# Turning q and k in three units instead of one, with q's second copy made by a transfer inside SBUF

## Chip, cores and metric

The kernel runs on one core of a Trainium2 chip (trn2). The metric is the device time of one execution in microseconds (us); of the kernel before it is the median of three runs.

## What is computed

One residual block over 4096 tokens of width 1024: a norm with a scale and shift from a conditioning vector, one projection into q, k, v, u and z, chunked attention over q, k, v, a trailing pool over u, a gate by silu(z), and an output projection. The change lies in the attention.

```python
h = rms_norm(x, norm_g) * (1 + scale) + shift
q, k, v, u, z = split(h @ w_in)          # q, k, v: 8 heads of 64
q = rms_norm(q, q_norm_g); k = rms_norm(k, k_norm_g)
# a chunk of 64 tokens attends to itself and to 8 chunks left of it
s = einsum('bqhd,bkhd->bhqk', qn, kn) * scale + bias
a_out = einsum('bhqk,bkhd->bqhd', softmax(s), vn)
y = concat([a_out, p_out]) * silu(z)
x = x + gate * (y @ w_out)
```

The inputs are float32. Each matmul operand is kept as a high part and a low part (the rest), both in the format fp32r, and a product is made of three matmuls: high by high, high by low, low by high.

## The kernel before

The program has three parts. From 0 to about 600 us the input is normed and transposed, u, z and the pool are made, and h goes to HBM as `hT_d`. From about 600 to 1730 us the attention runs. What is left of the output projection follows.

**Units.** The attention has two phases of four heads each; a phase has eight groups of 512 tokens. A unit `u` is one head on one group: 64 units, and group g of the 16 (both phases counted through) has the units 4g to 4g+3. The loop over `u` merges three lists of work into one order: the second half of unit u (probabilities transposed on TensorE, L623, cast to a high part on ScalarE, L629, and a low part on VectorE, L630, multiplied with v, L641 and L642), the first half of unit u+1 (scores, L583 and L584, into one PSUM tile `sps` that has no second buffer; bias and minimum on VectorE, L588; exponent on ScalarE, L601), and `work`, mostly one projection block of 128 tokens of a later group (L495 to L497). A projection block loads its h by SP (L105) and splits it (L96 on ScalarE, L97 on POOL); its q and k are normed by POOL and VectorE and stay in `qkr` tiles of the pool `b_qk`. The scheduler of the language then reorders the instructions and gives every engine one fixed order.

**Turns.** The scores need q and k with the 64 head dimensions on the partitions. `tq(which, pair)` does that for a pair of heads and one group, and is called a turn here: four transposes on TensorE (L537) of four `qkr` tiles into one PSUM tile, then for both heads (`s0`, `s1`: the two halves of the partitions)

```python
qs[s0] = copy(ps[s0])                    # L545, ScalarE, for q
qs[s1] = copy(ps[s0])                    # L546, ScalarE, the same values into the other half
ql[s0] = ps[s0] - qs[s0]                 # L548, VectorE, low part
ks[s0] = copy(ps[s0]); ks[s1] = ps[s0] - ks[s0]   # L556 ScalarE, L557 VectorE, for k
```

k's high part stands in one half of the partitions and its low part in the other, so one matmul with `qs` in both halves (L583) adds q-high by k-high and q-high by k-low; L584 with `ql` adds the third product. L583 therefore reads both copies of q. A group has four turns (q and k of two pairs). They stand in unit 4g-2, put into the projection block's items at every fifth place, and are ready for unit 4g, whose scores are made in the merged work of unit 4g-1.

**Buffers.** k lies in a ring of three slots of 512 tokens for each head; `slot` is the group modulo 3. A score tile covers 640 keys: where the group's slot is not the first of the ring, these lie side by side, and it is made of two pieces of 320 columns; where it is the first, of two pieces that together have 640 columns and whose sizes depend on the tile (512 and 128 for the first). `qs` has two buffers, `ql` one (two for the last head).

**Queues.** Every DMA that the program issues in the attention part stands in SP's queue, in order: loads of h (L105), loads of the gate tile z (L649), stores of y (L334), the bias (L461), and at the ends of the two phases the next weights (L125 and L139 for the projection, L408 for the output). An instruction that waits in that queue holds those behind it. A load of h into the staging buffer `bhr` (two buffers) waits until L97 has read the one before.

## Time and profile before

| | |
|---|---|
| median of three runs | 1998.72 us (1996.77 to 2001.21) |
| the profiled execution | 1996.48 us |
| its span, first to last instruction | 1994.6 us |
| mean granted clock of TensorE | 0.998 of full speed (2.4 GHz) |
| busy share of the span: TensorE matmuls | 97% |
| busy share: VectorE / ScalarE / POOL | 57% / 47% / 43% |

PE stands for TensorE's matmuls, PEld for its weight loads, which run beside matmuls; DVE is VectorE, ACT ScalarE, SP the engine that issues the DMAs. Matmuls are pipelined, and a PE row's ends are modelled. A window row gives a stretch of the trace: its bounds and length in us, then for each engine busy us and the number of instructions, the granted clock (1.00 is full speed), and the DMA share.

### The profile page before, as it was taken

How to read it: one execution, taken by the hardware profiler on the slowest of the kernel's cores; microseconds unless marked ns; L12 is line 12 of the kernel's file. 1: busy time of each engine (PE TensorE's matmuls, PEld its weight loads, DVE VectorE, ACT ScalarE, POOL GpSimd, SP SyncE). 2: the span in 40 equal slices, each digit the busy share in tenths (PEclk: the TensorE clock that was granted, in tenths of full speed). 3: DMA queues.
4: the chain of work that ended last, by engine and by line, in shares of the span. 5: the costliest groups of instructions: out<-in, count | busy, mean ns of one | idle time of the engine just before them, and what ended most of it. 6: DMA issues, size and time to landing. Idle time of an engine off the chain costs nothing.

```text
span 1994.6 us, 30020 instructions
## 1 busy us (share of the span) xinstructions
PE 1930.3 (97%) x10544; PEld 1657.0 (83%) x10544; DVE 1143.5 (57%) x2331; ACT 934.8 (47%) x1974; POOL 851.5 (43%) x1424
## 2 busy tenths in 40 slices
PE   6989999999999999999999999999999999999999
PEld 5778888888888888889888888898889788888887
DVE  7655654465635656666677666666666754333323
ACT  4422212221325656665678566756675864310121
POOL 7231332033045644445445656354445554422243
PEclk9999999999999999999999999999999999999999
DMA  9555344444431111111113222111111344544454
GB/s 331 192 174 159 103 135 145 141 123 141 148 101 53 59 58 33 44 54 43 54 52 97 74 60 64 33 59 38 43 54 43 101 142 139 180 136 149 146 181 164
DMA packets 167112, 211.76 MB, mean 106 GB/s; under 512 B 16432, under 2 KB 92720, under 8 KB 166960
## 3 DMA queue, kind: packets, MB, share of 16 engines
q1 hardware_dynamic: 166960, 209.84, 32.7%
q8 instruction: 83, 1.36, 0.3%
q14 instruction: 69, 0.57, 0.1%
HBM read 151.05 MB, written 58.74 MB: 105 GB/s over the span
## 4 chain that ended last, share of the span: by engine, by line
PE 85%; ACT 6%; DMA 3%; DVE 2%; POOL 2%; issue 2%; SPq 0%; ACTq 0%; POOLq 0%; DVEq 0%
PE ps L495 9%; PE ps L496 9%; PE ps L497 8%; PE ps L430 6%; PE ps L428 6%; PE ps L429 6%; PE ptps L623 5%; PE aps L297 4%; PE aps L298 4%; PE aps L296 4%; PE ps L297 4%; PE ps L298 4%; PE ps L296 4%; PE ops L641 3%; PE ops L642 3%; PE sps L583 3%
## 5 line engine op out<-in xcount | busy, mean ns | idle before, releaser
L97 POOL TENSOR_TENSOR bhl<-bhr,bhh 128x512 fp32r<-128x512 f32 x212 | 275.0, 1297 | 321.5 <-ACT bhh L96 313.5
L495 PE MATMUL ps<-w,bhh 128*128 128x512 f32 (+1 forms) x1024 | 353.6, 345 | 4.8 <-ACT qkr L508 4.6
L496 PE MATMUL ps<-w,bhh 128*128 128x512 f32 (+1 forms) x1024 | 352.5, 344 | 0.0
L497 PE MATMUL ps<-w,bhl 128*128 128x512 f32 (+1 forms) x1024 | 352.4, 344 | 0.0
L630 DVE TENSOR_TENSOR ptl<-ptps,pth 128x512 fp32r<-128x512 f32 x480 | 226.3, 486 | 145.6 <-ACT pth L629 142.1
L96 ACT CAST bhh<-bhr 128x512 fp32r<-128x512 f32 x224 | 138.9, 620 | 291.5 <-PE ps L429 184.9
L629 ACT CAST pth<-ptps 128x512 fp32r<-128x512 f32 x480 | 193.1, 425 | 147.2 <-PE ptps L623 132.3
L588 DVE CUSTOM_DVE_ANT_0 p<-sps,nb 128x640 f32<-128x640 f32 (+4 forms) x256 | 199.1, 778 | 86.4 <-PE sps L584 81.0
L601 ACT ACTIVATE p<-p,mx 128x640 f32<-128x640 f32 (+4 forms) x256 | 204.5, 799 | 90.7 <-DVE mx L588 89.6
L495 PEld LDWEIGHTS ps<-w,bhh 128*128 128x128 f32 x1024 | 193.7, 189 | 26.1 <-ACT qkr L508 7.9
L623 PE MATMUL ptps<-ident,p 128*128 128x128 f32 x1200 | 208.0, 274 | 3.5 <-DVE ql L548 2.9
L496 PEld LDWEIGHTS ps<-w,bhh 128*128 128x128 f32 x1024 | 193.7, 189 | 17.8
L497 PEld LDWEIGHTS ps<-w,bhl 128*128 128x128 f32 x1024 | 193.6, 189 | 17.2
L428 PE MATMUL ps<-w,bhh 128*128 128x512 f32 x512 | 200.6, 392 | 1.0 <-ACT bhh L96 1.0
L430 PE MATMUL ps<-w,bhl 128*128 128x512 f32 x512 | 200.3, 392 | 0.6 <-POOL bhl L97 0.6
L429 PE MATMUL ps<-w,bhh 128*128 128x512 f32 x512 | 200.2, 391 | 0.0
L259 POOL TENSOR_TENSOR xt<-xt,rb 128x512 f32<-128x512 f32 x56 | 80.0, 1463 | 234.2 <-DMA rb<-rs_d 234.2
L583 PE MATMUL sps<-kr,qs 128*128 128x320 f32 (+2 forms) x480 | 156.6, 334 | 13.0 <-DVE mx L588 12.3
L623 PEld LDWEIGHTS ptps<-ident,p 128*128 128x128 f32 x1200 | 144.3, 140 | 22.4 <-DVE ql L548 4.2
L641 PE MATMUL ops<-pth,v 128*128 128x512 f32 x480 | 157.7, 329 | 5.0 <-ACT pth L629 4.8
L642 PE MATMUL ops<-ptl,v 128*128 128x512 f32 x480 | 155.6, 334 | 0.1
L297 PE MATMUL aps<-hlo,w 128*128 128x512 f32 x392 | 153.6, 392 | 1.8 <-DVE hlo L97 1.8
(131 smaller groups left out, 3933.1 us busy)
## 6 DMA issues: line engine op xcount, KB each, us to landing
bhr<-hT_d SPq DMA_DIRECT2D x128, 256.0 KB, 2.7
bhr<-yT_d SPq DMA_DIRECT2D x96, 256.0 KB, 2.8
xt<-in_x_dram SPq DMA_DIRECT2D x32, 512.0 KB, 4.9
qkr<-in_x_dram SPq DMA_DIRECT2D x64, 256.0 KB, 3.4
out_dram<-qkr SPq DMA_DIRECT2D x64, 256.0 KB, 2.1
xt<-in_xT_dram SPq DMA_DIRECT2D x28, 512.0 KB, 6.5
hT_d<-xt SPq DMA_DIRECT2D x56, 256.0 KB, 2.3
w_s<-in_w_adaT_dram SPq DMA_DIRECT2D x16, 512.0 KB, 6.7
```

The lines of the kernel that those rows point to most:

```text
L97: eng.tensor_tensor(lo, raw, hi.bitcast(F32), op=ALU.subtract)
L297: nc.tensor.matmul(ps, wh[:, cs], l_, start=False, stop=False)
L428: nc.tensor.matmul(ps, a_, wh, start=k == 0, stop=False)
L429: nc.tensor.matmul(ps, a_, wl, start=False, stop=False)
L430: nc.tensor.matmul(ps, l_, wh, start=False, stop=k == KT - 1)
L495: nc.tensor.matmul(ps, a_, wh, start=k == 0, stop=False)
L496: nc.tensor.matmul(ps, a_, wl, start=False, stop=False)
L497: nc.tensor.matmul(ps, l_, wh, start=False, stop=k == KT - 1)
L583: nc.tensor.matmul(o, QS[ph, sg, h][:, qc], ks[:, k0 : k0 + n], start=True, stop=False)
L623: nc.tensor.transpose(out=ps[:, i * P : (i + 1) * P], in_=Pt[ph, sg, h, i][:, w : w + P], identity=ident)
L630: nc.vector.tensor_tensor(l_[:, r], ps[:, r], a_[:, r].bitcast(F32), op=ALU.subtract)
L641: nc.tensor.matmul(o[:, r], v, a_[:, r], start=n == 0, stop=False, skip_group_check=True)
```

## The change

The turns of a group are taken apart: q and k of pair 0 stay in unit 4g-2, q of pair 1 goes to unit 4g-1, k of pair 1 to unit 4g, by a table `turns`. (Group 0 keeps all four in one block.) q's second copy, ScalarE's L546, becomes a DMA from one half of the SBUF tile to the other, issued by SP: 64 x 512 values of 4 bytes, 128 KB, 64 times. `qs` has one buffer instead of two, the last head's `ql` one instead of two, the ring two slots instead of three; `b_qk` has eight buffers instead of six, since `qkr` tiles live longer. The gate tiles of the output get memory of their own.

```diff
-    op = ctx.enter_context(tc.tile_pool(name="b_qk", bufs=6))
+    op = ctx.enter_context(tc.tile_pool(name="b_qk", bufs=8))
...
-        qp = cb.enter_context(tc.tile_pool(name="b_q", bufs=2))
+        qp = cb.enter_context(tc.tile_pool(name="b_q", bufs=1))
...
-        ring = [kp.tile([P, 3 * SG], F32R, name=f"kr{h}") for h in range(HP)]
-        qlo = [[kp.tile([P, SG], F32R, name=f"ql{h}_{i}") for i in range(2 if h == HP - 1 else 1)] for h in range(HP)]
+        ring = [kp.tile([P, 2 * SG], F32R, name=f"kr{h}") for h in range(HP)]
+        qlo = [kp.tile([P, SG], F32R, name=f"ql{h}") for h in range(HP)]
...
         def slot(ph, sg):
-            return (ph * NSG + sg) % 3
+            return (ph * NSG + sg) % 2
...
                         nc.scalar.activation(qs[s0], ps[s0], AF.Copy, scale=gqn[s0])
-                        nc.scalar.activation(qs[s1], ps[s0], AF.Copy, scale=gqn[s0])
-                        ql = qlo[2 * pair + e][(ph * NSG + sg) % len(qlo[2 * pair + e])]
+                        nc.sync.dma_start(qs[s1].bitcast(F32), qs[s0].bitcast(F32))
+                        ql = qlo[2 * pair + e]
...
-            return [lambda w=w, p=p: tq(w, p) for p in range(2) for w in range(2)]
+            return {(w, p): (lambda w=w, p=p: tq(w, p)) for p in range(2) for w in range(2)}
...
-            if kb[1] >= 4 and kb[1] % 4 == 0:
-                for n, f in enumerate(tq_items(kb[0], kb[1] // 4 - 1)):
-                    it.insert((2 if kb != (0, 4) else 9) + (5 if kb != (0, 4) else 3) * n, f)
+            if kb == (0, 4):
+                t = tq_items(0, 0)
+                for n, wp in enumerate(((0, 0), (1, 0), (0, 1), (1, 1))):
+                    it.insert(9 + 3 * n, t[wp])
             return it
+        turns = {u: [] for u in range(-1, 64)}
+        for g in range(1, 2 * NSG):
+            t = tq_items(g // NSG, g % NSG)
+            turns[4 * g - 2] += [t[0, 0], t[1, 0]]
+            turns[4 * g - 1] += [t[0, 1]]
+            turns[4 * g] += [t[1, 1]]
...
-            if u in (26, 58):
-                work = [none] * 6 + [f for t in tq_items(u // 58, NSG - 1) for f in (t, none, none)] + work
-            if u == 27:
-                work = [none] * 20 + work
+            if u in (26, 27):
+                work = [none] * (16 if u == 26 else 20) + work
+            for n, f in enumerate(turns[u]):
+                work.insert(min(len(work), 3 + 6 * n), f)
...
-                    gate[n] = ring[n][:, SG : 2 * SG].bitcast(F32)
+                    gate[n] = bp.tile([P, 512], F32, name=f"gate{n}")
```

After the change a line behind L471 has the number of the line before less one (the first copy is L544, the transfer L545). Below, the rows that each engine runs in order, of both kernels.

ScalarE (ACT), group 11, from the first copy of q's pair 0 on. `qs00` is q for head 0 of pair 0 and `qs01` for its head 1, `kr0` the ring of head 0, `pth` a high part of probabilities, `p` the exponent, `bhh` the high part of h. Before:

```order
L545 ACTIVATE qs00_14511<-ptps_14506,gqn_4532 64x512
L546 ACTIVATE qs00_14511<-ptps_14506,gqn_4532 64x512
L96 CAST bhh_15320<-bhr_15318 128x512
L629 CAST pth_14529<-ptps_14525 128x384
L601 ACTIVATE p_14556,ls_14504<-p_14556,mx_14557 128x640
L629 CAST pth_14547<-ptps_14544 128x256
L545 ACTIVATE qs01_14515<-ptps_14506,gqn_4532 64x512
L546 ACTIVATE qs01_14515<-ptps_14506,gqn_4532 64x512
L556 ACTIVATE kr0_4534<-ptps_14560,pt_107 64x512
L601 ACTIVATE p_14630,ls_14504<-p_14630,mx_14631 128x640
```

After:

```order
L544 ACTIVATE qs00_14515<-ptps_14510,gqn_4532 64x512
L96 CAST bhh_15318<-bhr_15316 128x512
L544 ACTIVATE qs01_14519<-ptps_14510,gqn_4532 64x512
L628 CAST pth_14478<-ptps_14473 128x512
L628 CAST pth_14490<-ptps_14485 128x512
L600 ACTIVATE p_14499,ls_14502<-p_14499,mx_14500 128x640
L628 CAST pth_14527<-ptps_14523 128x384
L628 CAST pth_14542<-ptps_14539 128x256
L628 CAST pth_14567<-ptps_14563 128x384
L507 COPY qkr_15251<-ps_15168 128x512
L600 ACTIVATE p_14554,ls_14502<-p_14554,mx_14555 128x640
L555 ACTIVATE kr0_4534<-ptps_14599,pt_107 64x512
```

The second copies L546 are gone; casts of probabilities (L628) that stood behind the turn now stand between its copies. The first copy of pair 1 (`qs10_14757`) now stands 26 rows behind that of pair 0, the first copy of k for pair 1 another 18 rows on.

SP's queue at the end of phase 0, where the next phase's weights are loaded (eight loads L125, then four L139). `yT_d` is a store of y, `gzb` a load of the gate tile. Before:

```order
L125 DMA bhr_10949<-in_w_in_dram 128x2x256
L125 DMA bhr_10953<-in_w_in_dram 128x2x256
L125 DMA bhr_10959<-in_w_in_dram 128x2x256
L125 DMA bhr_10963<-in_w_in_dram 128x2x256
L334 DMA yT_d5_90<-osum_10254 128x4x128
L649 DMA gzb_11220<-gz_d6_83 128x512
L139 DMA bhr_10969<-in_w_in_dram 128x2x256
```

After:

```order
L125 DMA bhr_10947<-in_w_in_dram 128x2x256
L125 DMA bhr_10951<-in_w_in_dram 128x2x256
L125 DMA bhr_10957<-in_w_in_dram 128x2x256
L545 DMA qs10_10301<-qs10_10301 64x512
L125 DMA bhr_10961<-in_w_in_dram 128x2x256
L545 DMA qs11_10305<-qs11_10305 64x512
L139 DMA bhr_10967<-in_w_in_dram 128x2x256
```

Between the loads of the weights now stand the two transfers of q's pair 1 of group 6 (`qs10_10301`, `qs11_10305`). At the end of phase 1 the two of group 14 stand in the same way behind ten loads L408.

SP's queue in the turn of group 2, after the change (the `L105` rows before them are loads of h for group 4):

```order
L105 DMA bhr_7455<-hT_d4_73 128x512
L105 DMA bhr_7505<-hT_d4_73 128x512
L545 DMA qs00_6411<-qs00_6411 64x512
L105 DMA bhr_7688<-hT_d4_73 128x512
L334 DMA yT_d1_86<-osum_6126 128x4x128
L545 DMA qs01_6415<-qs01_6415 64x512
L648 DMA gzb_7178<-gz_d2_79 128x512
L545 DMA qs10_6653<-qs10_6653 64x512
L545 DMA qs11_6657<-qs11_6657 64x512
```

Before, the queue has only the rows L105, L334 and L649 here. The transfer `qs00_6411` stands behind two loads L105, each of which waits for a staging buffer. Between the last transpose of this q and the first score matmul that reads it TensorE has 37 instructions in its order; the other groups' counts are 29 (group 0), 43 (group 10) and 73 to 134.

## Rows read from the trace of the kernel before

**Rows 1.** Page, busy time (us), share of the span, instructions, by engine.

```profile
PE 1930.3 (97%) x10544; PEld 1657.0 (83%) x10544; DVE 1143.5 (57%) x2331; ACT 934.8 (47%) x1974; POOL 851.5 (43%) x1424
```

**Rows 2.** Windows: one turn stretch (group 11) and the stretch after it.

```profile
core 0: us, PE busy (x) PEld busy (x) DVE busy (x) ACT busy (x) POOL busy (x), PEclk, DMA share, GB/s
1342.90:1362.10 19.20, 16.70 (x97) 13.41 (x96) 15.84 (x36) 17.59 (x36) 3.79 (x7) 1.00 0.17 50
1362.10:1381.20 19.10, 19.10 (x131) 17.58 (x130) 11.96 (x27) 10.20 (x26) 12.21 (x30) 1.00 0.09 30
```

**Rows 3.** Windows: three of the twelve turn stretches, and the sum of twelve.

```profile
742.70:762.20 19.50, 16.96 (x94) 13.45 (x95) 15.97 (x36) 17.27 (x35) 1.95 (x5) 1.00 0.09 28
...
1210.60:1224.70 14.10, 13.85 (x84) 11.73 (x83) 10.44 (x26) 11.97 (x27) 7.13 (x17) 1.00 0.12 37
...
1548.60:1566.10 17.50, 15.85 (x93) 12.99 (x92) 13.65 (x30) 16.37 (x33) 3.86 (x6) 1.00 0.16 46
sum 221.80, PE 198.93 PEld 162.37 DVE 177.78 ACT 198.61 POOL 51.36; mean PE 16.58 PEld 13.53 DVE 14.82 ACT 16.55 POOL 4.28
```

**Rows 4.** Windows: one of ten stretches between turns, and the sum of ten.

```profile
1362.10:1411.80 49.70, 49.70 (x331) 45.62 (x330) 29.39 (x71) 26.79 (x66) 28.34 (x65) 1.00 0.15 46
...
sum 486.80, PE 485.93 PEld 443.00 DVE 293.22 ACT 272.95 POOL 278.52; mean PE 48.59 PEld 44.30 DVE 29.32 ACT 27.29 POOL 27.85
```

**Rows 5.** Windows: where weights are loaded (two), and between them a turn stretch.

```profile
1036.00:1077.10 41.10, 40.61 (x271) 36.18 (x269) 31.09 (x76) 31.89 (x76) 26.55 (x51) 1.00 0.36 109
1077.10:1099.90 22.80, 22.80 (x144) 20.32 (x142) 16.08 (x31) 18.12 (x34) 13.28 (x25) 1.00 0.22 70
1566.10:1601.70 35.60, 32.69 (x216) 28.61 (x215) 28.00 (x69) 29.57 (x72) 25.03 (x43) 1.00 0.43 133
```

**Rows 6.** Groups by line and shape: the copies and subtractions of the turns.

```profile
L545 ACT ACTIVATE qs<-ptps,gqn 64x512 fp32r<-64x512 f32 x64 | 43.6, 682 | 6.5 <-PE ptps L537 3.6 <-DVE ql L548 1.9
L546 ACT ACTIVATE qs<-ptps,gqn 64x512 fp32r<-64x512 f32 x64 | 43.7, 683 | 0.8
L556 ACT ACTIVATE kr<-ptps,pt 64x512 fp32r<-64x512 f32 x64 | 43.7, 683 | 4.6 <-PE ptps L537 1.9 <-DVE kr L557 1.3
L548 DVE SCALAR_TENSOR_TENSOR ql<-ptps,gqn,qs 64x512 fp32r<-64x512 f32 x64 | 47.9, 749 | 37.5 <-ACT qs L546 37.2
L557 DVE SCALAR_TENSOR_TENSOR kr<-ptps,pt,kr 64x512 fp32r<-64x512 f32 x64 | 48.0, 750 | 11.2 <-ACT kr L556 10.0
```

**Rows 7.** Waits, whole program: engine, line, releaser: us, times, longest.

```profile
DVE ql L548 <- ACT qs L546: 37.2, 41, 2.4
```

**Rows 8.** Groups by line and shape: score matmuls, by columns of a piece.

```profile
L583 PE MATMUL sps<-kr,qs 128*128 128x320 f32 x288 | 93.5, 332 | 8.1 <-DVE mx L588 7.5 <-DVE kr L557 0.3
L584 PE MATMUL sps<-kr,ql 128*128 128x320 f32 x288 | 88.1, 313 | 0.0
L583 PE MATMUL sps<-kr,qs 128*128 128x512 f32 x48 | 21.2, 442 | 1.8 <-DVE mx L588 1.8
L584 PE MATMUL sps<-kr,ql 128*128 128x512 f32 x48 | 18.9, 394 | 0.0
L583 PE MATMUL sps<-kr,qs 128*128 128x128 f32 x48 | 11.9, 248 | 0.0
L584 PE MATMUL sps<-kr,ql 128*128 128x128 f32 x48 | 13.2, 275 | 0.0
```

**Rows 9.** DMA issues: KB each, median us from issue to landing.

```profile
gz_d<-gz SPq DMA_DIRECT2D x32, 256.0 KB, 2.1
gzb<-gz_d SPq DMA_DIRECT2D x32, 256.0 KB, 2.9
```

**Rows 10.** Waits of SP's queue, 600 to 1630 us.

```profile
SPq L105 <- POOL bhl L97: 374.6, 63, 23.0
```

**Rows 11.** Timeline of SP: the end of the first weight loads.

```profile
1019.08 34.36 SPq L125 DMA_DIRECT2D bhr<-in_w_in_dram  x8
```

More of the change, by code (lines that the diff above doesn't have):

```diff
@@ L469, in block_kernel @@
         gk = pt[:, C_GK : C_GK + 1]
-        ring = [kp.tile([P, 3 * SG], F32R, name=f"kr{h}") for h in range(HP)]
-        qlo = [[kp.tile([P, SG], F32R, name=f"ql{h}_{i}") for i in range(2 if h == HP - 1 else 1)] for h in range(HP)]
+        ring = [kp.tile([P, 2 * SG], F32R, name=f"kr{h}") for h in range(HP)]
+        qlo = [kp.tile([P, SG], F32R, name=f"ql{h}") for h in range(HP)]
         for h in range(HP):
             z = slice((1 - h % 2) * HD, (2 - h % 2) * HD)
-            for t_ in qlo[h]:
-                nc.gpsimd.memset(t_[z].bitcast(F32), 0.0)
+            nc.gpsimd.memset(qlo[h][z].bitcast(F32), 0.0)
         def slot(ph, sg):
-            return (ph * NSG + sg) % 3
+            return (ph * NSG + sg) % 2
         Vt, QK, QS, QL = {}, {}, {}, {}
```

## The prediction

> **What bounds the kernel now.** I read the page's busy shares first. TensorE's matmuls fill 97% of the span, and no other engine reaches 60% [rows 1]. By that row at most 3% is left to win, and a reader would stop here. The second view, busy time by stretches, says where this misleads. Two neighbouring stretches of 19 us, cut at the units' borders, both at full clock: in the one without turns TensorE runs 131 matmuls and loads weights for 17.58 us; in the one with group 11's turns, as long, it runs 97 and loads for 13.41 [rows 2]. A weight load's time depends on what is loaded and not on who is late, so its share tells how dense the work is. Over ten stretches between turns it is 443.00/486.80 = 0.910 [rows 4]; there the other engines are at 60% (VectorE), 56% and 57%, and matmuls fill 99.8%. Over twelve turn stretches it is 162.37/221.80 = 0.732 [rows 3]. At the density between turns their work would last 162.37/0.910 = 178.4 us, so the turns cost 221.8 - 178.4 = **43.4 us**, 3.6 each. What holds TensorE there is ScalarE: 17.59 of 19.20 us busy in the example, 198.61 of 221.80 in all (90%), with VectorE next at 80% [rows 2, 3].
>
> By the matmuls' idle time only 221.80 - 198.93 = 22.9 us are lost there [rows 3]. The Trainium skill ("Perfetto Trace Analysis", section "Identifying the Most-Contended Engine") says that matmul busy time is a poor measure of the distance to the limit, since matmuls are pipelined, and that the busy share of weight loads is a better one. This trace agrees: 16.70 against 19.10 us of matmuls, but 97 against 131 of them [rows 2].
>
> **What goes from the turn stretches.** Of a group's turns, ScalarE has 12 copies (4 L545, 4 L546, 4 L556) of 0.683 us, VectorE 8 subtractions of 0.750 us [rows 6]. The four second copies become transfers. Of pair 1, two first copies of q and two copies of k go to the next two units, with four subtractions and eight transposes. So a turn stretch loses 8 x 0.683 = 5.46 us of ScalarE, 4 x 0.750 = 3.0 us of VectorE, and of TensorE 8 x 0.15 = 1.2 us (the pace between turns, 49.70 us for 331 matmuls [rows 4]). Over twelve stretches: ScalarE 198.6 - 65.6 = 133 us, VectorE 177.8 - 36 = 142 us, TensorE 178.4 - 14.4 = 164 us. ScalarE falls to 81% of TensorE's need, VectorE to 86%: TensorE bounds the stretch again, with less slack than elsewhere. The waits of the subtraction for the second copy, 37.2 us in all [rows 7], go too, since in the changed order L547 waits for the first copy alone; they lie inside the 43.4 and are not added.
>
> **What stays lost there.** Nothing before has exactly this load; I bound it by the nearest rows, each with the same 0.910. The turn stretch by the weight loads (ScalarE 79%, VectorE 71%) needs 20.32/0.910 = 22.3 of its 22.8 us, 2% lost; the weights of phase 0 (78% and 76%) 36.18/0.910 = 39.8 of 41.1, 3%; the weights of phase 1 (83%, 79%) 28.61/0.910 = 31.4 of 35.6, 12% [rows 5]; group 8's turn stretch, in which only part of the turns lies (85%, 74%), 11.73/0.910 = 12.9 of 14.1, 9% [rows 3]. I take 9% of 164 = **14.8 us**, since this row is a turn stretch with eight transposes as each will be; ends 3 us (2%) and 20 us (12%). The gain is 43.4 - 14.8 = 28.6 us.
>
> **What the neighbours take.** The two units after the turn get 4 x 0.683 = 2.7 us of ScalarE and 3.0 us of VectorE in each group. Over 49.7 us ScalarE rises from 56% to about 61%, VectorE from 60% to 66%, below every row above that loses time: nothing. TensorE's 1.2 us are moved, not saved. If this cover fails (the scores' single buffer waits for a VectorE that is late), 1% of 487 us is 5 us.
>
> **The ring.** With two slots, 8 groups instead of 9 have their keys side by side (of 14 that have keys to the left; 288 pieces of 320 columns are 9 groups of 16 tiles of 2 pieces [rows 8]). In the other one, 16 tiles take split pieces: 0.442 + 0.394 + 0.248 + 0.275 = 1.36 us for the most uneven against 2 x (0.332 + 0.313) = 1.29. That is at most 16 x 0.07 = 1.1 us; I take 0.6. The buffers that are gone (q, low part, ring slot) hold nobody up in the built order: q of pair 0 is written when heads 0 and 1 of the group before have long been read. The two `qkr` buffers more give room for turns that read later.
>
> **The transfer's latency.** q's first copy used to be followed by the second, 0.68 us; now by a transfer. No row has one inside SBUF; those of 256 KB land 2.1 and 2.9 us after issue [rows 9], and this one is half as large. The first score needs it, and TensorE's 37 instructions between (group 2; 29 and 43 for groups 0 and 10) are 4.4 to 6.5 us of work at 0.15; all other groups have 11 us or more. Copy and landing need 0.7 + 2.9 = 3.6 us, so these three fit if SP issues at once. But the transfer stands behind loads L105, which wait for POOL, 374.6 us in 63 waits: 5.9 us in the mean, 23.0 at most [rows 10]. With a wait of 5.9 us 3.6 + 5.9 = 9.5 us are needed: late by 5.1, 3.9 and 3.0, together 12 us; the others still have room. The loads ahead are freed by TensorE's work 12 to 34 rows before the transposes, so I expect most of the wait to be over: **3 us**, ends 0 and 12.
>
> The Trainium skill ("SBUF — State Buffer", section "Door 1: The DMA port swizzle") has a rule against this part: a transfer of 64 partitions reaches half of the 16 ports. No row shows such a transfer. As an estimate by that page it lasts as long as a full one of twice the size, so one takes the 2.9 us of the 256 KB rather than less, up to 0.8 us more, 2.4 us at the three tight turns.
>
> **The phase ends.** There the transfers of pair 1 stand between weight loads, eight L125 in 34.36 us, 4.3 us for each [rows 11]. q of pair 1 is needed 65 to 113 instructions after its transposes (9.8 to 17 us): two loads ahead are covered, a third is not. I take **3 us** for both ends, ends 0 and 12.
>
> **Sum.** 43.4 - 14.8 - 0.6 - 3 - 3 = 22.0 us off the profiled execution of 1996.48: 1974.5. It stands 2.2 us below the median of the runs, so the forecast for the median is **1976.7 us**. With all low ends it is 1998.7 - 40.4 = 1958; with all high ends 43.4 - 20 - 1.1 - 12 - 12 is a loss of 2, 2000.
>
> **Rivals.**
> - *Nearly all stalls go* (chance 0.09): the turns lose nothing, and the later turn of pair 1 also relieves the weight stretches, which lose 1.3 and 4.2 us now. 43.4 - 1 + 3 = 45: 1953 us. For it: stretches with ScalarE at 79% lose 2% [rows 5].
> - *VectorE takes ScalarE's place* (0.17). It is left with 86% of TensorE's need, 95% in the fuller stretches ((15.84 - 3.0)/(14.7 - 1.2) for group 11 [rows 2]), and the scores wait for it. With 12%, 20 us, left in the turn stretches, 1% in the neighbours (5 us) and 10 us of latency instead of 6: 43.4 - 20 - 5 - 10 - 0.6 = 8 us of gain: 1991.
> - *Matmul idle time is the true measure* (0.06): only 22.9 us could be won, and 22.9 - 14.8 - 6.6 = 1.5: 1997. Against it are the counts of matmuls.
> - *SP's queue decides* (0.10), slower. If the loads ahead wait w at each turn, each transfer is late by 3.6 + w less its room (4.4, 5.6 and 6.5 us for the tight groups, 11 to 20 for the rest). At w = 13 the sum is 62 us over the 16 groups, against 43.4 - 14.8 - 0.6 - 3 = 25 won without it: 37 slower, 2036. It passes no change near w = 9.4, where the lateness is some 26 us. Mean wait 5.9 and longest 23.0 [rows 10] leave this possible; that L105's waits mostly end before the turn's transposes speaks against.
> - That the change does not do what it says is excluded by the built order: 64 transfers in SP's queue, no second copy on ScalarE.
>
> **Numbers.** The forecast's own case has 0.58. Some 0.2% (4 us) is what a measurement of this kernel can tell from no change. Faster by more: forecast, all stalls gone, VectorE, less 0.02 for their upper tails: 0.82. Within 0.2%: the matmul-idle case and those tails, 0.08. Slower: SP's queue, 0.10. The range leaves out the slower rival and half of the fastest, and reaches over the VectorE case to the idle-time case: 1953 to 1998 us.
>
> **What would show it.** Right: in the turn stretches the weight loads' share rises from 0.73 to about 0.83, ScalarE falls from 90% to about 75%; L546's 43.7 us are gone, the wait for the second copy with it; pieces of 320 columns fall from 288 to 256. Wrong: scores waiting for the DMA of `qs` for more than some 6 us in all (SP's queue); scores waiting longer for L588 with VectorE over 90% in the turn units (VectorE); a longer lateness at the two phase ends; or turn stretches as long as before with fewer matmuls.

## The result, and the profile after

The changed kernel takes 1988.79 us (median of 4 runs, 1987.33 to 1990.24) against 1999.53 us of the kernel before beside it (4 runs): a ratio of 0.9948, 95% interval 0.9930 to 0.9965. That is 10.7 us less, where 22 had been forecast: the direction holds and the time lies inside the range, but the gain is half the size. The profiled execution took 1987.33 us, with a span of 1985.0 us, 9.6 less than before.

The page's busy row, which answers to [rows 1]:

```profile
PE 1932.2 (97%) x10544; PEld 1659.5 (84%) x10544; DVE 1139.5 (57%) x2331; ACT 892.0 (45%) x1910; POOL 852.1 (43%) x1423
```

TensorE still stands at 97%. ScalarE has lost 42.8 us, nearly all of the second copies' 43.7, and VectorE 4.0.

Busy time by stretches (the columns as in [rows 2]). First the units 4g-2 of the same twelve groups as in [rows 3], with the example of group 11 and the sum:

```profile
1342.40:1355.00 12.60, 12.06 (x89) 10.91 (x87) 9.73 (x23) 9.20 (x21) 5.91 (x14) 1.00 0.13 42
...
sum 158.80, PE 151.35 PEld 132.32 DVE 124.65 ACT 122.26 POOL 94.02; mean PE 12.61 PEld 11.03 DVE 10.39 ACT 10.19 POOL 7.83
```

At the density of [rows 4] (weight-load time over length) the weight loads need 132.32/0.910 = 145.4 us, so 158.8 - 145.4 = 13.4 us are lost here, where it was 43.4. Now the units 4g-1 behind them, which the prediction had taken for free, after the change: those of groups 6, 8, 11 and 14, then the sum of the twelve.

```profile
1030.20:1048.60 18.40, 16.99 (x99) 14.29 (x99) 13.54 (x32) 15.03 (x36) 6.59 (x6) 1.00 0.40 113
1165.10:1188.30 23.20, 21.57 (x126) 18.45 (x127) 14.87 (x41) 13.84 (x38) 8.19 (x12) 1.00 0.18 50
...
1355.00:1376.60 21.60, 21.32 (x134) 18.76 (x133) 15.93 (x35) 14.73 (x36) 6.64 (x8) 1.00 0.11 29
...
1560.30:1573.00 12.70, 11.19 (x66) 8.72 (x65) 10.95 (x28) 12.44 (x31) 7.03 (x7) 1.00 0.45 134
sum 224.10, PE 216.58 PEld 187.04 DVE 156.72 ACT 153.33 POOL 65.61; mean PE 18.05 PEld 15.59 DVE 13.06 ACT 12.78 POOL 5.47
```

and the sum of the same twelve units in the kernel before:

```profile
sum 223.40, PE 222.43 PEld 202.80 DVE 146.42 ACT 128.19 POOL 154.09; mean PE 18.54 PEld 16.90 DVE 12.20 ACT 10.68 POOL 12.84
```

Before, 223.4 - 202.80/0.910 = 0.5 us were lost in them; now it is 224.1 - 187.04/0.910 = **18.6 us**. The two kinds of unit together lost 43.9 us and now lose 32.0: 11.9 us gained, 30 in the one and 18 given back in the other. Of the 18.6 us, 8.7 lie in three of the twelve units: those of groups 6 and 14, where weights are loaded, and that of group 8, the last unit of phase 0.

How the loss divides between the two kinds is less sure than their sum, since the density also depends on what TensorE does. Two stretches of projection matmuls alone, without a gap, show it: of 256 columns (v), then of 512 (q and k).

```profile
1269.60:1271.70 2.10, 2.10 (x20) 2.10 (x19) 2.06 (x7) 1.31 (x5) 0.79 (x1) 1.00 0.00 0
1425.80:1430.10 4.30, 4.30 (x20) 3.55 (x19) 2.62 (x8) 2.24 (x6) 0.00 (x0) 1.00 0.25 51
```

Their densities are 1.00 and 0.83, both with nothing lost. The units 4g-1 had 467 projection matmuls of 256 columns and 308 of 512 before, and 231 and 350 after, so part of their lower density is a different mix of work. An estimate that gives each kind of matmul the time that it takes in the stretches of [rows 4] puts these units at 2 us lost before and 14 after, and the units 4g-2 at 32 and 14.

Where in those units the time goes is seen in a finer cut around group 11. All engines:

```profile
1342.40:1351.00 8.60, 8.60 (x66) 8.10 (x64) 6.55 (x14) 6.17 (x14) 2.74 (x4) 1.00 0.01 2
1351.00:1360.00 9.00, 8.17 (x51) 6.65 (x51) 8.15 (x22) 7.93 (x20) 4.61 (x13) 1.00 0.25 73
1360.00:1376.60 16.60, 16.60 (x106) 14.92 (x105) 10.96 (x23) 9.83 (x23) 5.20 (x5) 1.00 0.10 29
```

and the first of the three projection lines (L494) alone, with its count in brackets:

```profile
1342.40:1351.00 8.60, 2.33 (x8) 1.51 (x8) 1.00 0.01 2
1351.00:1360.00 9.00, 0.00 (x0) 0.00 (x0) 1.00 0.25 73
1360.00:1376.60 16.60, 7.59 (x21) 3.98 (x21) 1.00 0.10 29
```

Between 1351 and 1360 us TensorE has no projection matmul at all, and there, in 9 us, it loads weights for 6.65 us (0.74), while VectorE is busy for 8.15 and ScalarE for 7.93. In the stretches on both sides, with projections, the density is 0.94 (mostly projections of 256 columns) and 0.90 (of 512). The 9 us lie across the border of the two units, at 1355.0: they begin in unit 4g-2 and end in 4g-1. The same holds before: from 1342.9 to 1356.2 us one projection matmul of that line ran. So the stretch has become shorter and less costly, but it has not gone. What stands at its two ends is the timeline of ScalarE (start, length, line; rows of the projection's results alone):

```profile
1329.90 0.59 ACT L507 COPY qkr<-ps 128x512 f32<-128x512 f32 x1
...
1345.04 0.59 ACT L507 COPY qkr<-ps 128x512 f32<-128x512 f32 x1
...
1356.17 0.27 ACT L96 CAST v<-ps 128x128 fp32r<-128x128 f32 x1
...
1360.60 0.24 ACT L96 CAST v<-ps 128x128 fp32r<-128x128 f32 x1
...
1371.09 0.59 ACT L507 COPY qkr<-ps 128x512 f32<-128x512 f32 x1
```

The v of two projected blocks (L96 into `v`) is copied out between 1356.2 and 1360.8 us, though the last matmul of the later block ended at 1350.8; the copy of q and k (L507) at 1371.09 comes 3.9 us after its block's matmuls. The projection has two PSUM tiles (the pool `pp` has two buffers), and both then hold a v. That these wait for one of v's 14 buffers is borne out by e1 below.

What the prediction said of the parts. The groups by line and shape, which answer to [rows 6] and [rows 8]:

```profile
L544 ACT ACTIVATE qs<-ptps,gqn 64x512 fp32r<-64x512 f32 x64 | 43.7, 683 | 9.1 <-DVE ql L547 4.5 <-PE ptps L536 3.7
...
L555 ACT ACTIVATE kr<-ptps,pt 64x512 fp32r<-64x512 f32 x64 | 43.6, 681 | 9.7 <-PE ptps L536 5.7 <-DVE kr L556 3.4
...
L582 PE MATMUL sps<-kr,qs 128*128 128x320 f32 x256 | 82.5, 329 | 3.9 <-DVE mx L587 3.5
```

the wait that answers to [rows 7], the wait of SP's queue for the first copies, and the DMA issues (KB each, us to landing):

```profile
DVE ql L547 <- ACT qs L544: 11.3, 17, 1.7
```

```profile
SPq L545 <- ACT qs L544: 52.7, 30, 9.4
```

```profile
gzb<-gz_d SPq DMA_DIRECT2D x32, 256.0 KB, 3.1
qs<-qs SPq DMA_DIRECT2D x64, 128.0 KB, 2.3
```

L546 is gone, the subtraction's wait fell from 37.2 us (for the second copy) to 11.3 (for the first), and pieces of 320 columns from 288 to 256. A transfer lands 2.3 us after issue; no wait of TensorE for a DMA of `qs` is in the trace.

### The profile page after: what moved, and what is told of

Same layout as the page of the kernel before. It is cut to its first block, busy times and chain, and to the rows that moved or that the text cites. A ratio compares the mean times of both kernels' runs of the same rounds, so it can differ in the third digit from the quotient of the medians.

```text
span 1985.0 us, 30104 instructions
## 1 busy us (share of the span) xinstructions
PE 1932.2 (97%) x10544; PEld 1659.5 (84%) x10544; DVE 1139.5 (57%) x2331; ACT 892.0 (45%) x1910; POOL 852.1 (43%) x1423
## 4 chain that ended last, share of the span: by engine, by line
PE 88%; DVE 5%; DMA 3%; ACT 2%; issue 1%; POOL 1%; SPq 0%; DVEq 0%; POOLq 0%; ACTq 0%
PE ps L494 9%; PE ps L495 9%; PE ps L496 9%; PE ps L430 6%; PE ps L429 6%; PE ps L428 6%; PE ptps L622 6%; PE aps L297 4%; PE aps L298 4%; PE aps L296 4%; PE ps L297 4%; PE ps L298 4%; PE ps L296 4%; PE sps L582 3%; PE ops L641 3%; PE ops L640 3%
## 5 line engine op out<-in xcount | busy, mean ns | idle before, releaser
L494 PE MATMUL ps<-w,bhh 128*128 128x512 f32 (+1 forms) x1024 | 354.3, 346 | 2.7 <-ACT qkr L507 2.5
L96 ACT CAST bhh<-bhr 128x512 fp32r<-128x512 f32 x224 | 138.7, 620 | 283.6 <-PE ps L429 177.7
L628 ACT CAST pth<-ptps 128x512 fp32r<-128x512 f32 x480 | 193.8, 425 | 136.9 <-PE ptps L622 111.2
L622 PE MATMUL ptps<-ident,p 128*128 128x128 f32 x1200 | 213.0, 274 | 0.3
L494 PEld LDWEIGHTS ps<-w,bhh 128*128 128x128 f32 x1024 | 193.5, 189 | 21.7 <-ACT qkr L507 3.6
L640 PE MATMUL ops<-pth,v 128*128 128x512 f32 x480 | 162.7, 340 | 4.1 <-ACT pth L628 2.6
```

The source lines that it names most:

```text
L494: nc.tensor.matmul(ps, a_, wh, start=k == 0, stop=False)
L622: nc.tensor.transpose(out=ps[:, i * P : (i + 1) * P], in_=Pt[ph, sg, h, i][:, w : w + P], identity=ident)
L640: nc.tensor.matmul(o[:, r], v, a_[:, r], start=n == 0, stop=False, skip_group_check=True)
```

## The experiments

All times are medians beside runs of the kernel before on the same chip; the third column is the difference to those. Every kernel is within 2% of the one before, so the intervals decide what can be told apart.

| kernel | us | to before, us | ratio, 95% interval |
|---|---|---|---|
| changed | 1988.79 | -10.7 | 0.9948, 0.9930 to 0.9965 |
| e1: 16 buffers for v | 1986.61 | -12.1 | 0.9941, 0.9928 to 0.9953 |
| e3: six buffers for qkr | 1986.84 | -11.8 | 0.9946, 0.9934 to 0.9959 |
| e4: spread, second copy on ScalarE | 1995.92 | -2.8 | 0.9988, 0.9979 to 0.9997 |
| e5: before, with the transfer alone | 1986.25 | -12.4 | 0.9936, 0.9923 to 0.9950 |
| e6: 17 for v, ten for qkr | 1982.91 | -16.9 | 0.9914, 0.9900 to 0.9927 |
| e7: changed, pinned, eight | 2002.66 | +2.8 | 1.0012, 1.0003 to 1.0021 |
| e8: before, pinned, eight | 1994.27 | -5.6 | 0.9970, 0.9959 to 0.9982 |
| e9: changed, pinned, two | 1992.94 | -6.9 | 0.9962, 0.9950 to 0.9975 |
| e10: k's copy short | 1985.86 | -12.6 | 0.9938, 0.9925 to 0.9950 |
| e11: k's subtraction short | 1988.45 | -10.0 | 0.9950, 0.9937 to 0.9964 |
| e12: as e9, border free | 1985.67 | -12.7 | 0.9936, 0.9923 to 0.9948 |
| e13: before, turns light | 1972.16 | -26.8 | 0.9869, 0.9854 to 0.9884 |
| e14: changed, turns light | 1977.23 | -21.7 | 0.9890, 0.9877 to 0.9904 |
| e15: as e14 and e12 together | 1987.24 | -11.7 | 0.9943, 0.9931 to 0.9955 |
| e16: spread over two units | 1983.32 | -16.6 | 0.9910, 0.9896 to 0.9923 |
| e17: as e16, 18 for v, nine for qkr | 1976.70 | -23.3 | 0.9880, 0.9866 to 0.9893 |

**One part at a time (e5, e4), and the buffers (e1, e3).** The first theory after the result was that v's buffers hold the projections back (theory V); its rival, the prediction's own, that the engines' load does (theory A).

```diff
 e1, from the changed kernel
-        vp = cb.enter_context(tc.tile_pool(name="b_v", bufs=14))
+        vp = cb.enter_context(tc.tile_pool(name="b_v", bufs=16))
 e3, from the changed kernel
-    op = ctx.enter_context(tc.tile_pool(name="b_qk", bufs=8))
+    op = ctx.enter_context(tc.tile_pool(name="b_qk", bufs=6))
 e4, from the changed kernel (e5 is the reverse of it, from the kernel before)
-                        nc.sync.dma_start(qs[s1].bitcast(F32), qs[s0].bitcast(F32))
+                        nc.scalar.activation(qs[s1], ps[s0], AF.Copy, scale=gqn[s0])
```

> The changed kernel with 16 buffers for v instead of 14. Theory V (buffers): in the changed kernel the projected v of two blocks in each group waits for a v buffer (21.4 and 9.8 us for blocks 50 and 51), both PSUM tiles of the projection are then full, and TensorE has no projection matmuls to fill the attention's waits (none from 1350.8 to 1360.6 us). With 16 buffers the two waits fall under 5 us and the time falls by 15 to 30 us against the changed kernel: 1959 to 1974. Theory A (load): ScalarE and VectorE, busy to 77 to 98% in the units of the turns, hold TensorE whatever the buffers: within 4 us of the changed kernel's 1989.

> The changed kernel with six qkr buffers again instead of eight. Theory V: the copy of a block's q and k (L507) waits for the last turn of its group, as in the kernel before (19.3 us for block 50), and now longer, since k of pair 1 is turned a unit and a half later: slower than the changed kernel by 10 us or more, at or above the kernel before (1995 to 2015). Theory A: the engines' work is the same, so within 4 us of 1989.

> The changed kernel with q's second copy on ScalarE again, no transfer inside SBUF. Theory V: ScalarE's 2.7 us more in each group lie beside the wait for v buffers: 0 to 5 us slower than the changed kernel, 1989 to 1994. Theory A: ScalarE is what holds TensorE in those units, 15 groups of 2.7 us come back, most of them in the open: 2005 or more.

> The kernel before with only q's second copy made by the transfer inside SBUF. Theory V: block 4n+2's qkr still waits for the group's last turn and its v for a buffer, so TensorE still lacks projection matmuls: 0 to 6 us faster than the kernel before, 1993 to 1999. Theory A: 2.7 us of ScalarE go from each of 15 groups where ScalarE is over 90% busy: 20 to 35 us faster, 1965 to 1980.

Theory V failed on both buffers: two more for v won nothing that can be told (1.4 us, intervals overlap), two fewer for qkr lost nothing. The built order sends projections ahead until some buffer is full, and the wait turns up at the next one: from 660 to 1560 us the copies of v that start over 2 us behind their block's last matmul wait 373 us in sum in the changed kernel and 62 in e1, those of q and k 43 and 307. In e1's ScalarE timeline:

```profile
1334.47 0.59 ACT L507 COPY qkr<-ps 128x512 f32<-128x512 f32 x1
...
1341.34 0.25 ACT L96 CAST v<-ps 128x128 fp32r<-128x128 f32 x1
...
1361.17 0.26 ACT L96 CAST v<-ps 128x128 fp32r<-128x128 f32 x1
...
1372.91 1.07 ACT L507 COPY qkr<-ps 128x512 f32<-128x512 f32 x2
```

the v casts follow their blocks by 3 to 6 us, and the copy of q and k (two in one row) at 1372.91 waits instead, 25.7 us after the matmuls of block 52.

The parts did tell something: the transfer alone (e5) wins 12.4 us, the spread with its buffers alone (e4) 2.8, between the forecasts of the two theories, both together 10.7. So **the transfer alone wins as much as the whole change**, and what the spread adds to it is nothing or a loss. ScalarE's work counts, as theory A has it, but less than it said: 43.7 us of ScalarE taken away are 12.4 us of time, not 20 to 35. In e5 the stretch of group 11 without projections reads

```profile
1334.00:1344.00 10.00, 9.00 (x61) 7.87 (x60) 9.04 (x21) 9.17 (x20) 3.73 (x5) 1.00 0.49 138
```

10.0 us long (13.3 before), with ScalarE and VectorE at 92% and 90% and a density of 0.79, against 9.0 us and 0.74 with the spread. The spread shortened it by 1 us and made it no denser.

The units tell what the spread does. The same sums as above for other kernels, cut at each one's own borders, and the losses by the density of 0.910:

| kernel | units 4g-2 lose, us | units 4g-1 lose, us | together, us | time to before, us |
|---|---|---|---|---|
| before | 43.4 | 0.5 | 43.9 | |
| e4: spread alone | 14.1 | 23.5 | 37.6 | -2.8 |
| changed | 13.4 | 18.6 | 32.0 | -10.7 |
| e5: transfer alone | 26.2 | 3.2 | 29.4 | -12.4 |
| e16 | 13.8 | 13.8 | 27.6 | -16.6 |
| e17 | 18.4 | 2.7 | 21.1 | -23.3 |
| e14 | 7.2 | 14.2 | 21.4 | -21.7 |

The sums of both kinds follow the times to within 3.5 us. With all of the turns' work in three units, e4 and the changed kernel lose 23.5 and 18.6 us in units 4g-1; e5, without the spread, loses 3.2. The experiments e14, e16 and e17 are told further down: e14 halves the turns' work, e16 and e17 spread it over two units. The rows of e5, e14 and e17, each for 4g-2 and for 4g-1:

```profile
sum 191.70, PE 179.87 PEld 150.62 DVE 169.31 ACT 160.15 POOL 56.58; mean PE 14.99 PEld 12.55 DVE 14.11 ACT 13.35 POOL 4.72
sum 236.90, PE 233.36 PEld 212.68 DVE 153.38 ACT 139.45 POOL 153.46; mean PE 19.45 PEld 17.72 DVE 12.78 ACT 11.62 POOL 12.79
```

```profile
sum 146.70, PE 140.52 PEld 126.95 DVE 107.99 ACT 106.06 POOL 88.30; mean PE 11.71 PEld 10.58 DVE 9.00 ACT 8.84 POOL 7.36
sum 227.00, PE 221.61 PEld 193.64 DVE 148.79 ACT 146.56 POOL 68.07; mean PE 18.47 PEld 16.14 DVE 12.40 ACT 12.21 POOL 5.67
```

```profile
sum 194.30, PE 187.09 PEld 160.08 DVE 134.28 ACT 138.96 POOL 52.91; mean PE 15.59 PEld 13.34 DVE 11.19 ACT 11.58 POOL 4.41
sum 247.30, PE 246.30 PEld 222.55 DVE 193.94 ACT 171.06 POOL 149.98; mean PE 20.53 PEld 18.55 DVE 16.16 ACT 14.25 POOL 12.50
```

**Keeping the projections among the attention (e6 to e9, e12).** If TensorE stalls where projections are missing, an order that cannot run ahead should cure it (theory G).

```diff
 e7 (LAG 8), e9 (LAG 2), from the changed kernel; e8 (LAG 8), from the kernel before
+                with tc.issue_after(pvs[-LAG].ins) if len(pvs) > LAG else nullcontext():
                     nc.tensor.matmul(ps, a_, wh, start=k == 0, stop=False)
...
+                pvs.append(nc.tensor.matmul(o[:, r], v, l_[:, r], start=False, stop=last, skip_group_check=True))
 e12, from e9
+                with tc.issue_after(pvs[-LAG].ins) if len(pvs) > LAG and (ph == 0 or b >= 6) else nullcontext():
 e6, from the changed kernel: b_v bufs=17, b_qk bufs=10
```

> The changed kernel with both kinds of buffers deeper: 17 for v (14), ten for qkr (8). With 16 for v alone the stall moved: v no longer waited, but block 52's qkr waited 25.7 us for the group's last turn. Theory B (buffers): with both deeper the projection-free stretches, 136.8 us in the changed kernel, fall under 80 and the time falls by 10 to 20 us, to 1969 to 1979. Theory G (run ahead): the built order sends the projections ahead until any buffer is full, then TensorE has none left while it waits for the lump that the group frees; more buffers only move the stretches: 110 to 150 us of them remain, 1982 to 1990.

> The changed kernel, with every projection matmul kept in TensorE's order behind the PV matmul that stands eight PV matmuls before it in the program, so that projections cannot run ahead. Work and buffers are as in the changed kernel. Theory G: the projection-free stretches of 9 to 19 us go (the built order has one over 4 us left), and with them most of the 34 us of stall in them: 1955 to 1970. Theory A (load of ScalarE and VectorE in the units with turns): the same instructions on the same engines in the same units, 1984 to 1992. Slower than 1992 if the order kept makes TensorE wait for projections' inputs.

> The kernel before with the same pinning of the projections and nothing of the change: all four turns in one unit, both copies of q on ScalarE. Theory G: the stretches without projections (154.6 us, 48.5 us of stall in them) mostly go: 1955 to 1975, faster than the changed kernel. Theory A: ScalarE is still over 90% busy in the units of the turns: 1990 to 2002.

> As the pinned changed kernel, but each projection matmul behind the PV matmul two before it, so that projections follow the attention more closely. Theory G: as with eight, within 5 us of it. If the distance matters, the closer one is slower, since a projection that is late for its input then holds the attention's matmuls behind it.

> The changed kernel with projections pinned two PV matmuls back, except for the first six blocks of phase 1, which may run ahead again. Pinned throughout, it lost 13.1 us at 1050 to 1100 us, at the phases' border, where the changed kernel loses 1.5, and won inside the phases (22.5 us of stall against 35.2 in 700 to 1050 and 1200 to 1550 us). Theory G2 (attention alone, without projections among it, runs at the pace of ScalarE and VectorE): without the border's loss 9 to 13 us faster than pinned throughout, 1980 to 1984, and so 5 to 9 faster than the changed kernel. If the spacing of the projections does not matter: no better than the changed kernel, 1987 to 1993.

As a forecast of the time theory G failed. Pinned to eight the changed kernel is slower than before; pinned to two it is no better than unpinned, though 10 us faster than with eight, where within 5 us or slower had been expected. The kernel before, pinned (e8), gains 5.6 us, in theory A's range. Inside a phase e9 spreads the work well, as its stretches of 16 us show (PE, PEld, DVE, ACT, POOL):

```profile
1312.00:1328.00 16.00, 15.43 (x100) 13.58 (x100) 9.52 (x22) 10.01 (x23) 8.18 (x18) 1.00 0.25 74
1328.00:1344.00 16.00, 15.46 (x101) 13.83 (x99) 11.88 (x29) 11.65 (x27) 6.33 (x17) 1.00 0.22 58
1344.00:1360.00 16.00, 16.00 (x107) 14.66 (x106) 11.19 (x26) 9.94 (x23) 9.60 (x19) 1.00 0.22 67
```

The density is 0.85, 0.86 and 0.92 with ScalarE at 62 to 73%: there is no long stretch without projections, and yet some is lost in the first two rows, in which TensorE is busy for 15.4 of 16 us and three of the group's four turns stand. Freeing the border of the phases (e12) brought 1985.7, between its two forecasts and no better than the transfer alone. Where the pinning wins and loses shows in sums of windows, first of 700 to 1050 and 1200 to 1550 us, inside the phases, then of 640 to 700 and 1050 to 1110, at the start of each; in each pair the changed kernel, then e12:

```profile
sum 700.00, PE 689.24 PEld 612.50 DVE 464.22 ACT 439.34 POOL 344.81; mean PE 344.62 PEld 306.25 DVE 232.11 ACT 219.67 POOL 172.40
sum 700.00, PE 691.84 PEld 621.71 DVE 470.17 ACT 446.46 POOL 338.79; mean PE 345.92 PEld 310.86 DVE 235.09 ACT 223.23 POOL 169.39
```

```profile
sum 120.00, PE 118.86 PEld 105.75 DVE 75.16 ACT 70.20 POOL 74.67; mean PE 59.43 PEld 52.88 DVE 37.58 ACT 35.10 POOL 37.34
sum 120.00, PE 113.95 PEld 97.89 DVE 76.66 ACT 76.87 POOL 67.08; mean PE 56.98 PEld 48.95 DVE 38.33 ACT 38.44 POOL 33.54
```

Inside the phases e12 loads 9.2 us more of weights in the same time: there the filling does pay. At their starts it loads 7.9 us less, and most of the gain is lost again. Why the starts lose is open. Deeper buffers of both kinds (e6) gave 6 us more than the change: the time is at the low end of theory G's range and outside theory B's, and the long stretches without projections, 91.5 us in sum where the changed kernel has 136.8, lie between the two ranges for them.

**Which engine's work (e10, e11, e13 to e15).** With VectorE at 91% and ScalarE at 88% of the 9 us, the rival of the prediction, VectorE in ScalarE's place, stood open.

```diff
 e10
-                        nc.scalar.activation(ks[s0], ps[s0], AF.Copy, scale=gk[s0])
+                        nc.scalar.activation(ks[s0, 0:P], ps[s0, 0:P], AF.Copy, scale=gk[s0])
 e11
-                            ks[s1], ps[s0], gk[s0], ks[s0].bitcast(F32), op0=ALU.mult, op1=ALU.subtract
+                            ks[s1, 0:P], ps[s0, 0:P], gk[s0], ks[s0, 0:P].bitcast(F32), op0=ALU.mult, op1=ALU.subtract
 e13 (before), e14 (changed): the same for every copy and subtraction of the turns; e15: e14 with e12's pinning
```

The columns that these kernels leave out stay zero, so only their times count. In e13 to e15 `qs` also lies in tiles of its own, as many as its buffers were. The transfers of e14 and e15 still move all 512 columns.

> The changed kernel, with k's first copy on ScalarE on 128 of its 512 columns (k's high part is left at zero in the rest of the columns). Some 64 x 0.4 = 26 us less of ScalarE, nothing else. In the changed kernel's stretches without projections VectorE is busy for 94% and ScalarE for 92%. Theory D (VectorE has taken ScalarE's place): 0 to 3 us faster than the changed kernel. Theory S (ScalarE still sets the pace): 8 to 15 us faster. Theory B2 (both pace it by turns): 3 to 8 us faster, and the same for the other one.

> The changed kernel, with k's subtraction on VectorE on 128 of its 512 columns (k's low part is left at zero in the rest). Some 64 x 0.46 = 29 us less of VectorE, nothing else. Theory D: 8 to 15 us faster than the changed kernel. Theory S: 0 to 3 us faster. Theory B2: 3 to 8 us.

> The kernel before, with the copies and subtractions of all turns on 128 of their 512 columns (the rest of q and k is left at zero): some 79 us less of ScalarE and 59 us less of VectorE, the transposes unchanged. The prediction's premise (theory T: the 43.4 us of the turn stretches are caused by the turns' work on ScalarE): 30 to 43 us faster than the kernel before, 1955 to 1969. Theory P (most of the stall belongs to attention that runs without projections among it, at its own pace, and the turns only add to it): 10 to 22 us faster, 1976 to 1988.

> The changed kernel, lightened in the same way: some 52 us less of ScalarE and 59 us less of VectorE. Theory T: 20 us or more faster than the changed kernel, 1968 or less. Theory P: 0 to 8 us faster, 1981 to 1989, with 8 or more stretches of 7 us and longer without projections still there and 1.2 to 2 us of stall in each.

> The lightened changed kernel with the projections pinned two PV matmuls back (border free). Theory P: what is left of the stall goes when both causes are gone, the missing projections and the turns' work: 10 to 20 us faster than the changed kernel, 1969 to 1979, and the stall inside the phases (700 to 1050 and 1200 to 1550 us) falls under 12 us, from 35. If the stall has another cause, it stays over 20 us there.

The shortened instructions, in e10, e11 and (two of five groups) e13:

```profile
L557 ACT ACTIVATE kr<-ptps,pt 64x128 fp32r<-64x128 f32 x64 | 23.1, 361 | 14.1 <-PE ptps L538 9.3 <-DVE kr L558 4.0
```

```profile
L558 DVE SCALAR_TENSOR_TENSOR kr<-ptps,pt,kr 64x128 fp32r<-64x128 f32 x64 | 22.4, 350 | 17.3 <-ACT kr L557 15.8
```

```profile
L548 ACT ACTIVATE qz<-ptps,gqn 64x128 fp32r<-64x128 f32 x64 | 23.3, 363 | 0.8
...
L559 DVE SCALAR_TENSOR_TENSOR kr<-ptps,pt,kr 64x128 fp32r<-64x128 f32 x64 | 22.4, 350 | 15.2 <-ACT kr L558 13.6
```

They cost 0.36 and 0.35 us instead of 0.68 and 0.75, so that less was taken away than the expectations had: 20.5 us of ScalarE in e10, 25.6 us of VectorE in e11, some 61 and 51 us in e13, 41 and 51 in e14. Against the changed kernel e10 won 2 us, within the two intervals, and e11 nothing, so each of the three theories fails in one of the two at least: **neither k's copy nor k's subtraction alone is what holds TensorE now**. The rival's 1991 us was the nearest to the result; that VectorE's subtraction of k is the limit, as it would have it, is not borne out, and its other work was not tested alone. e13 won 26.8 us, between the two theories' ranges, and e14 11.0 on top of the change, above theory P's 8 and below theory T's 20; the unit table above has it losing 14.2 us in units 4g-1 still. So the turns' work on ScalarE and VectorE is worth its place in the prediction: taking half of it away in the kernel before is worth 26.8 us. It is worth this when it is *taken away*. e15, where both causes should have gone, missed by over 8 us: pinned, the light turns win nothing. Why was not found.

**Where the turns stand (e16, e17).**

```diff
 e16, from the changed kernel; e17 the same with b_v bufs=18, b_qk bufs=9
-            turns[4 * g - 1] += [t[0, 1]]
-            turns[4 * g] += [t[1, 1]]
+            turns[4 * g - 1] += [t[0, 1], t[1, 1]]
```

> The changed kernel with both turns of pair 1 in unit 4g-1 (spread over two units instead of three). If where the turns stand is worth nothing, as the transfer alone (1986.3) against transfer and spread (1988.8) suggests: 1984 to 1991. If the spread itself helps and a second unit gives half of it: 1992 or more. If the third unit is what harms (the qkr tiles are held until unit 4g): 1978 to 1984.

> The same with 18 buffers for v and nine for qkr: the search for a version that beats both. Deeper buffers gave 6 us with three units (1982.9); with two units the qkr tiles come free earlier, so the same or up to 4 us more: 1978 to 1983. Over 1985 if deeper buffers only moved the stretches without projections by luck of the built order.

With the turn of k of pair 1 one unit earlier the kernel takes 1983.3 us, 16.6 less than before; the interval, 0.9896 to 0.9923, lies below that of the changed kernel (0.9930 to 0.9965). The third unit of the spread is a loss. A likely reason, not shown, is that a `qkr` tile is held until the last turn has read it: from 660 to 1560 us the copy L507 started over 2 us behind its block's last matmul for nine blocks in the changed kernel, 43.3 us in sum (the one at 1371.09 above is one of them), and for one block, 3.1 us, in e16, while v's waits are no shorter (373 and 434 us). Against it stands that such waits do not order the times: q and k wait some 190 us in e5 and 306 in e17, the fastest of these. With deeper buffers as well (e17) it is **1976.7 us**, 1.3 under what was expected and 23.3 less than before: the version that beats both. Whether the kernel before, or e5, would have gained as much from such buffers was not run. The busy times from 660 to 1560 us, the third value of a row being that of the weight loads, in the kernel before, the changed one, e5, e16 and e17:

```profile
660.00:1560.00 900.00, 874.35 (x5560) 775.72 (x5558) 593.60 (x1404) 594.08 (x1332) 449.14 (x965) 1.00 0.18 54
```

```profile
660.00:1560.00 900.00, 884.87 (x5614) 785.55 (x5613) 595.70 (x1416) 562.79 (x1290) 466.17 (x1000) 1.00 0.22 64
```

```profile
660.00:1560.00 900.00, 881.51 (x5647) 787.78 (x5645) 612.81 (x1434) 571.86 (x1306) 458.83 (x987) 1.00 0.22 64
```

```profile
660.00:1560.00 900.00, 885.11 (x5645) 788.72 (x5643) 600.02 (x1429) 569.81 (x1305) 469.05 (x1003) 1.00 0.22 64
```

```profile
660.00:1560.00 900.00, 887.84 (x5657) 793.00 (x5656) 611.07 (x1427) 571.91 (x1309) 471.46 (x1009) 1.00 0.23 67
```

More weights loaded in the same 900 us is work that is further on: 775.7, 785.6, 787.8, 788.7 and 793.0, in the order of the five times.

## Why the prediction was right or wrong

- *ScalarE holds the turn stretches, and the second copies' end pays.* The second half is right: e5, the transfer alone, is 12.4 us faster, and the waits of [rows 7] fell as said. Whether ScalarE's load or the subtraction's wait behind the second copy was the cost, e5 can't tell: it ends both.
- *What stays lost there, 9% of 164 us = 14.8.* Right: 13.4 us by the same density, and 14 by the estimate from the kinds of matmul. The signs named for it came too: the weight loads' share of these units is 0.83, ScalarE's 77%.
- *What the neighbours take: nothing.* **This step failed.** It put 2.7 us of ScalarE and 3.0 of VectorE per group on 49.7 us of neighbours whose mean load is 61 and 66%, and priced them at 0. The term measured 18.1 us (18.6 after, 0.5 before), or 12 by the estimate from the kinds of matmul. The work does not fall on the mean: 26.2 of the 32.8 us of ScalarE and 25.5 of the 36.0 us of VectorE that were moved in these twelve groups stand in unit 4g-1, into which the attention without projections reaches. With the spread the long stretches without projections reach into these units, too: over 3 us long, they take 53 us of the twelve, and none in the kernel before and in e5. The work alone is not what it costs: e14 halves it, and 14.2 us stay lost. Nor do both together settle it: e17 has about as much work there (23.5 and 31.3 us) and 43 us of such stretches, and loses 2.7. So the loss is the spread's, as e4 and e5 show, but what makes it, and what deeper buffers change in it, stays open.
- With the terms as measured the sum is 43.4 + 0.5 - 13.4 - 18.6 = 11.9 us, against 9.6 of the span and 10.7 of the medians. The 43.4 itself may be too large: its reference of 0.910 belongs to another mix of matmuls, and the estimate from their kinds has 32.
- Behind it lies that half of the forecast gain was for work that is moved, not removed. e4 shows what moving alone is worth here, 2.8 us, and e16 that the move to a third unit costs more than it gives.
- *The transfer's latency, 3 us, and the phase ends, 3 us.* Both measured zero: no wait of TensorE for `qs` from a DMA is in the trace. SP's waits for the first copies are there, 52.7 us in 30 waits, but no score matmul is seen to wait for a second copy. The rival on SP's queue falls with them, and the two terms had hidden part of the error in the neighbours. The rule of the Trainium skill on 64 partitions ("SBUF — State Buffer", "Door 1: The DMA port swizzle"), that they reach only half of the 16 ports, is neither shown nor refuted by the transfer's own time: 2.3 us for 128 KB inside SBUF beside 3.1 for 256 KB from HBM, and no run tells a fixed part of these from the ports. The prediction's estimate by it, 2.9 us, was too long. It changed nothing in the sum, as nothing waited.
- *The ring.* As said: 256 pieces of 320 columns, and no new wait beside it.
- *Matmul idle time as the true measure.* Its sum, 1.5 us, failed, but by terms that it shared with the forecast. In the 24 units matmul idle time fell from 23.8 to 15.0 us, by 8.9, and the density gives 11.9 where the span fell by 9.6, so this change can't tell the two measures apart. e13 can: its span of 1970.1 us is 24.5 shorter, and its idle time, 1970.1 - 1920.3 = 49.8 us beside 1994.6 - 1930.3 = 64.3, only 14.5.
- *The built order shows what it does.* It did, but the prediction read only the places of the turns in it, and not where the projections are missing: in TensorE's order a run without projections can be seen before any run.

## What to carry to other kernels

Whether it pays to move work out of a stalled stretch is decided where the work lands: look there at the density in a window of some 10 us around the landing place, not at the mean over the units, and compare densities only of stretches with the same mix of matmuls. Removing the second copies paid 0.28 us for each us of ScalarE (12.4 of 43.7); moving as much paid a fraction of it (e4), and moving part of it a unit further cost more than it gave (e16). When a buffer is what stops the filler, making that one deeper can hand the wait to the next (e1): deepening both gave 6 us (e6), the shorter spread 6 (e16), and both steps together over 12 (e17).

## What was not expected of the hardware

A transfer of 64 x 512 values from one half of the partitions to the other landed in 2.3 us in the median, and 64 of them cost TensorE no wait. An instruction on a quarter of the columns is not a quarter of the time: 0.36 us on 128 columns against 0.68 on 512 on ScalarE, 0.35 against 0.75 on VectorE.
